# Delta rule in a two-layer network: the substitution of the diagonal blocks on GpSimd, fixed padded rows for the convolution, z's products tied to the inverse's last levels

## The chip, the cores and the metric

The kernel runs on one core of a Trainium2 chip. The metric is the time of the program on the device in microseconds (us). Three runs of the kernel before gave a median of 1310.2 us (1309.93 to 1312.19). Engines are called by their names in the profile: PE is TensorE's matmul side and PEld its weight loads, DVE is VectorE, ACT is ScalarE, POOL is GpSimd, SP is SyncE, which issues the loads of weights.

## The reference, cut to what matters

The whole program is a network with two mixers, several MLPs and a second block; the change lies in its first layer, a gated delta rule over 256 tokens, 8 heads of 128. There:

```python
proj = hn @ w_in                                   # q, k, v, z: 1024 columns each, and 16 gate columns
qkv = silu(causal_depthwise_conv(proj[..., :3 * DN_DIM], conv_w))
...
a_low = where(tri_strict, einsum('bhncd,bhnsd->bhncs', k_beta, k) * decay, 0.0)
a_mat = a_low + eye(c)
sol = triangular_solve(a_mat, rhs, lower=True, unit_diagonal=True)
...
o = rmsnorm(o, out_norm_g) * silu(z)
return o.reshape(b, t, DN_DIM) @ w_out
```

The triangular matrix needs k and the gates alone. The z columns are needed only where the output o is gated.

## The kernel before, in words

Everything of the delta rule is in `delta_net`. Its products with `w_in` run in three passes per weight tile (high and low halves of the fp32 operands), through `lin`, `group` and `mm3`. A group of 512 columns takes 96 products of 128x128x256, fed by four chunks of weights of 512 KB; each chunk costs an ACT copy (`wh`, L76) and a DVE subtraction (`wl`, L56) in `split`. Names in rows: `acc<-xh,wh` and its two companions are these products; `ps` is any other bank of PSUM.

The stages, in the order of the text:

1. `gates`, `decays`, then `project` of k (two groups), `unit_keys` and `gram`. `gram` leaves in A, for 4 heads times 2 chunks of 128 rows, the triangular matrices.
2. `inverses`: the inverse Z of A starts from its 32x32 blocks on the diagonal. Four DMAs (L573) of POOL's queue bring those out to HBM (`ga`), two more (L576) bring them back one block per partition (`at`). 31 steps of substitution follow, each of them a product into `tmp` and a subtraction from `zt`, 62 TENSOR_TENSOR of DVE in all, each of which needs the one ahead of it. Then `zt` goes out (`gz`, L594, two DMAs) and back into the diagonal of Z (L597, four DMAs).
3. Two levels, `level_64` and `level_128`, each for the four pairs of g and c, join the blocks: four transposes of Z on PE (`turned`, L603), an ACT copy into X, small products of Z with A, an ACT copy into Y, products of Y with X, an ACT copy back into Z.
4. `project` of q and v. Each pair of 128 columns goes through `conv_pair`: ACT copies it behind three zeros in a tile `pad` of the rotating pool (L507 is the POOL memset of those zeros, made anew for every pair), and six DVE operations (`cy`, L59) add up the taps.
5. `intra` (products of q with k), `tokens` (transposes of k and v), and the generator `outputs`, a chain of products, ACT copies and DVE operations per half g.
6. The two groups of z, `lin(W, KD, [(3072, 512)], rd, on_z)` and the one at 3584, with `on_z`: a DVE operation, three ACT operations and another DVE operation per pair of columns, which release the bank of PSUM. At the end `residual_lin` multiplies by `w_out` (192 products, `acc<-xoh` and `acc<-xh`), then the MLP starts.

The order on each engine isn't that of the text: a scheduler takes, engine by engine, what it holds to be ready, by priority (the order of the text, put back by `later(n)`), and `after(...)` puts an instruction behind a named one. Each engine then runs its list in order. With two banks, `acc`, for the products with weights, a group's first product waits until `on_z` or the convolution has read the bank.

Of the kernel before, what the change touches and what calls it, by code (L numbers as in the profile page):

```python
# [8 lines left out]
F32 = mybir.dt.float32  # L9
# [3 lines left out]
OP = mybir.AluOpType  # L13
# [3 lines left out]
P = 128  # L17
T = 256
# [6 lines left out]
class Net:  # L25
# [420 lines left out]
    def delta_net(self):  # L446
        nc, tc, a = self.nc, self.tc, self.a
# [4 lines left out]
        with ExitStack() as ctx:  # L452
            dp = ctx.enter_context(tc.tile_pool(name="dn", bufs=1, reuse_waits="tile"))
# [45 lines left out]
            A = core.tile([P, 16, P], F32, name="A")  # L499
            Z = core.tile([P, 16, P], F32, name="Z")  # L500
            nc.gpsimd.memset(Z, 0.0)
            four = lambda t, g, c: t[:, (g * 2 + c) * 4:(g * 2 + c) * 4 + 4, :]

            def conv_pair(col, o, dst, behind):
                t = col // P
                pad = dp.tile([P, 2, T + 3], F32, tag="pad", name="pad", bufs=2)
                nc.gpsimd.memset(pad[:, :, 0:3], 0.0)  # L507
                self.copy(pad[:, :, 3:], o)
                y = dp.tile([P, 2, T], F32, tag="cy", name="cy", bufs=2)
                w = lambda j, i: cw[:, j * 24 + t + i:j * 24 + t + i + 1]  # L510
                for i in range(2):
                    self.act(y[:, i, :], o[:, i, :], AF.Copy, scale=w(3, i))
                for j in range(3):
                    for i in range(2):
                        self.stt(y[:, i, :], pad[:, i, j:j + T], w(j, i), y[:, i, :], OP.mult, OP.add)
                with self.after(*behind):
                    self.last_silu = self.act(dst, y, AF.Silu)

            def project(dst, tag, base, g, behind):
                dst[g] = dp.tile([P, 4, T], F32, tag=tag, name=tag, bufs=2)  # L520
                base += g * 512
                self.lin(W, KD, [(base, 512)], rd, lambda col, o: conv_pair(
                    col, o, dst[g][:, (col - base) // P:(col - base) // P + 2, :], behind))

            def big(tag, bufs, pool=None):
                return (pool or core).tile([P, 4, P], F32, tag=tag, name=tag, bufs=bufs)
# [39 lines left out]
            def inverses(sv):  # L566


                ga = hbm.tile([4, 16, 32, 32], F32, name="ga")
                gz = hbm.tile([4, 16, 32, 32], F32, name="gz")  # L570
                for b in range(4):
                    r = slice(32 * b, 32 * b + 32)
                    nc.gpsimd.dma_start(ga[b].rearrange("m i j -> i m j"), A[r, :, r])  # L573
                at = sv.tile([P, 32, 32], F32, name="at")
                for s in range(2):
                    nc.gpsimd.dma_start(at[s * 64:s * 64 + 64], ga.rearrange("b m i j -> (b m) i j"))  # L576
                zt = sv.tile([P, 16, 32], F32, name="zt")
                zi = sv.tile([P, 16, 32], I32, name="zi")
                nc.gpsimd.iota(zi, pattern=[[-2, 16], [1, 32]], base=0, channel_multiplier=0)
                zf = sv.tile([P, 16, 32], F32, name="zf")  # L580
                nc.gpsimd.tensor_copy(zf, zi)
                for s in range(2):
                    r = slice(s * 64, s * 64 + 64)
                    self.ts(zt[r], zf[r], float(s), None, OP.is_equal, eng=nc.gpsimd)
                tmp = sv.tile([P, 160], F32, name="tmp")
                for j in range(31):
                    n, m = j // 2 + 1, 31 - j
                    u = tmp[:, 0:n * m].rearrange("p (c i) -> p c i", i=m)
                    self.tt(u, zt[:, 0:n, j:j + 1].to_broadcast([P, n, m]),
                            at[:, j + 1:32, j][:, None, :].to_broadcast([P, n, m]), OP.mult)  # L590
                    self.tt(zt[:, 0:n, j + 1:32], zt[:, 0:n, j + 1:32], u, OP.subtract)
                to = gz.rearrange("b m (c s) i -> s (b m) c i", s=2)
                for s in range(2):
                    nc.gpsimd.dma_start(to[s], zt[s * 64:s * 64 + 64])  # L594
                for b in range(4):
                    r = slice(32 * b, 32 * b + 32)
                    nc.gpsimd.dma_start(Z[r, :, r], gz[b].rearrange("m c i -> c m i"))  # L597

            def turned(zz):
                X = big("X", 2)  # L600
                p = self.ps()
                for i in range(4):
                    nc.tensor.transpose(p[:, i * P:(i + 1) * P], zz[:, i, :], self.ident)  # L603
                self.copy(X, v4(p))
                return X

            def level_64(A, zz):

                X = turned(zz)
                v = lambda p, r: p[r:r + 32, 0:128].rearrange("p (h e) -> p h e", e=32)  # L610
                Y = big("Y", 2)
                p = self.ps()
                for r in (0, 64):
                    for i in range(4):
                        self.mm(p[r:r + 32, i * 32:(i + 1) * 32], A[r + 32:r + 64, i, r:r + 32],
                                zz[r + 32:r + 64, i, r + 32:r + 64], True, True)
                    self.copy(Y[r:r + 32, :, 0:32], v(p, r))
                p = self.ps()
                for r in (0, 64):
                    for i in range(4):  # L620
                        self.mm(p[r:r + 32, i * 32:(i + 1) * 32], X[r:r + 32, i, r:r + 32], Y[r:r + 32, i, 0:32],
                                True, True)
                    self.act(zz[r:r + 32, :, r + 32:r + 64], v(p, r), AF.Copy, scale=-1.0)
# [15 lines left out]
            def intra(g, c):  # L639

                cs = slice(c * P, (c + 1) * P)
                m = M[g, c]
                self.tt(m, m, b4(self.tri[:, 0:P]), OP.mult)
                p = self.ps()
                mm4(p, lambda i: (k[g][:, i, cs], q[g][:, i, cs]))
                self.tt(m, v4(p), m, OP.mult)
                if c == 1:
                    self.tt(qd[g], q[g][:, :, cs], qd[g], OP.mult)

            def tokens(g):  # L650

                h4 = slice(g * 4, g * 4 + 4)
                for c in range(2):
                    cs = slice(c * P, (c + 1) * P)
                    p = self.ps()
                    for i in range(4):
                        nc.tensor.transpose(p[:, i * P:(i + 1) * P], k[g][:, i, cs], self.ident)
                    kx[c] = big(f"kx{c}", 1, late)
                    self.tt(kx[c], v4(p), tok((beg if c else kdec)[:, h4]), OP.mult)
                    p = self.ps()  # L660
                    for i in range(4):
                        nc.tensor.transpose(p[:, i * P:(i + 1) * P], vt[g][:, i, cs], self.ident)
                    bv[c] = big(f"bv{c}", 1, late)
                    self.tt(bv[c], v4(p), tok(beta[:, c, h4]), OP.mult)
# [63 lines left out]
            both = [(g, c) for g in range(2) for c in range(2)]  # L728
# [12 lines left out]
            with tc.tile_pool(name="inv", bufs=1, reuse_waits="tile") as sv:  # L741
                inverses(sv)
            late = ctx.enter_context(tc.tile_pool(name="late", bufs=1, reuse_waits="tile"))
            for level in (level_64, level_128):
                for g, c in both:
                    level(four(A, g, c), four(Z, g, c))
            project(q, "q", 0, 0, behind)
            project(q, "q", 0, 1, behind)
            project(vt, "vt", 2048, 0, behind)
# [1 line left out]
            pin = self.table(self.last_silu)  # L751
            for g, c in both:
                intra(g, c)
            tokens(0)
            step = lambda it: next(it, None)
            out = [outputs(g) for g in range(2)]
            step(out[0])
            with self.later(300):
                self.lin(W, KD, [(3072, 512)], rd, on_z)
            step(out[0])  # L760
            step(out[0])
            xo[0] = (late.tile([P, 4, T], F32R, name="xoh"), late.tile([P, 4, T], F32R, name="xol"))
            with self.later(600):
                self.lin(W, KD, [(3584, 512)], rd, on_z)
            xo[1] = self.new_xg(0)
            tokens(1)
# [779 lines left out]
```

## Time and profile before

| | |
|---|---|
| median of 3 runs | 1310.2 us |
| the profiled execution | 1310.08 us, of it 1308.3 us span |
| PE busy | 1261.0 us (96%) |
| DVE busy | 867.1 us (66%) |
| ACT busy | 737.8 us (56%) |
| POOL busy | 20.9 us (2%) |
| TensorE clock granted, mean | 0.977 of full speed |
| chain that ended last: PE, DVE, ACT | 86%, 6%, 3% |

The profile is of one execution. Busy times of PE are modelled and overlap, so a busy PE isn't a PE at its peak. A clock of 1.00 in a row is 2.4 GHz, 0.50 is 1.2 GHz. The change touches the time from 71 to 230 us of the span; the stage tables below cut it where the work of PE changes: the rest of k's, all of q's and v's products (71.6 to 102.5), the first of z's (102.5 to 109.9), a stretch with the rest of z's (109.9 to 144.8), the two levels of the inverse (144.8 to 173.2), q with k (173.2 to 178.3), tokens and outputs (178.3 to 210), the rest of the products with `w_out` (210 to 229.8).

### The profile page before, as it was taken

Reading aid. Unit: us, or ns where it says so; the run is one execution under the profiler, and the core shown is the slowest. Engines: PE = TensorE matmul, PEld = TensorE weight load, DVE = VectorE, ACT = ScalarE, POOL = GpSimd, SP = SyncE. Lnnn points to the kernel's source line nnn. Section 1 sums busy time; section 2 is a strip of 40 time slices with the busy share of each in tenths; the row PEclk is TensorE's granted clock in tenths of the full one; section 3 lists DMA queues with packets and bytes.
Section 4 is the critical chain, followed back from the end, with each engine's and each line's share of the span. In section 5 each row is a group of like instructions: output and inputs, shape, how many; then the busy total and the mean of one; then the engine's idle time right before and its main releaser. Section 6 shows DMA issues by size and latency. Waiting matters only on the chain.

```text
span 1308.3 us, 23770 instructions
## 1 busy us (share of the span) xinstructions
PE 1261.0 (96%) x9674; PEld 1199.7 (92%) x9674; DVE 867.1 (66%) x1385; ACT 737.8 (56%) x1124; POOL 20.9 (2%) x68
## 2 busy tenths in 40 slices
PE   7997789999999999999999999999999998999998
PEld 6997688999999999999999987899999997999997
DVE  5799236644547666744546997998556685877775
ACT  5874536645546445755545644675447565656554
POOL 2010100000000000000000000000000000000000
PEclk8998689999999999999999999999999999999999
DMA  6454303666664744656652653446664654465652
GB/s 199 143 171 145 81 1 129 219 196 187 183 182 141 216 153 143 210 166 181 188 166 64 194 162 87 139 131 192 183 188 148 208 161 129 132 205 170 184 177 84
DMA packets 99633, 207.32 MB, mean 158 GB/s; under 512 B 9694, under 2 KB 12292, under 8 KB 99524
## 3 DMA queue, kind: packets, MB, share of 16 engines
q1 hardware_dynamic: 98114, 202.85, 50.7%
q0 software_dynamic: 928, 2.88, 0.8%
q8 instruction: 76, 1.25, 0.4%
q14 instruction: 33, 0.27, 0.1%
q10 hardware_dynamic: 482, 0.08, 0.0%
HBM read 204.21 MB, written 1.57 MB: 157 GB/s over the span
## 4 chain that ended last, share of the span: by engine, by line
PE 86%; DVE 6%; ACT 3%; issue 2%; DMA 2%; POOL 0%; DVEq 0%; SPq 0%; ACTq 0%; POOLq 0%
PE acc L53 53%; PE ps L53 32%; DVE wl L56 1%; ACT wh L76 1%; PE ps L603 1%; DVE cy L59 1%; DVE tmp L56 1%; PE ps L893 0%; DVE zt L56 0%; DVE sq L56 0%; DMA wr<-in_w_xkv_dram 0%; DMA xt<-in_x_dram 0%; DMA Z<-gz 0%; DMA gz<-zt 0%; DVE mx L879 0%
## 5 line engine op out<-in xcount | busy, mean ns | idle before, releaser
L56 DVE TENSOR_TENSOR wl<-wr,wh 128x1024 fp32r<-128x1024 f32 (+1 forms) x384 | 465.6, 1217 | 308.2 <-ACT wh L76 307.3
L76 ACT ACTIVATE wh<-wr 128x1024 fp32r<-128x1024 f32 (+1 forms) x384 | 402.3, 1052 | 394.3 <-PE acc L53 246.9
L53 PE MATMUL acc<-xh,wh 128*128 128x256 f32 (+1 forms) x1064 | 305.9, 288 | 7.8 <-DVE z L59 5.1
L53 PE MATMUL acc<-xh,wl 128*128 128x256 f32 (+1 forms) x1064 | 303.8, 286 | 3.5 <-DVE wl L56 3.5
L53 PE MATMUL acc<-xl,wh 128*128 128x256 f32 (+1 forms) x1064 | 304.4, 286 | 0.8 <-DVE xl L56 0.8
L53 PE MATMUL ps<-xh,wh 128*128 128x256 f32 (+1 forms) x872 | 248.5, 285 | 6.7 <-ACT xh L69 3.5
L53 PE MATMUL ps<-xl,wh 128*128 128x256 f32 (+1 forms) x872 | 248.2, 285 | 0.5 <-DVE xl L56 0.3
L53 PE MATMUL ps<-xh,wl 128*128 128x256 f32 (+1 forms) x872 | 248.0, 284 | 0.0
L53 PEld LDWEIGHTS acc<-xh,wh 128*128 128x128 f32 (+1 forms) x1064 | 204.4, 192 | 11.4 <-issue 6.5
L53 PEld LDWEIGHTS acc<-xh,wl 128*128 128x128 f32 (+1 forms) x1064 | 204.1, 192 | 6.0 <-DVE wl L56 3.7
L53 PEld LDWEIGHTS acc<-xl,wh 128*128 128x128 f32 (+1 forms) x1064 | 204.6, 192 | 3.2 <-issue 1.5
L53 PEld LDWEIGHTS ps<-xh,wh 128*128 128x128 f32 (+1 forms) x872 | 166.8, 191 | 8.4 <-ACT xh L69 3.9
L53 PEld LDWEIGHTS ps<-xl,wh 128*128 128x128 f32 (+1 forms) x872 | 166.9, 191 | 1.6 <-DVE xl L56 1.1
L53 PEld LDWEIGHTS ps<-xh,wl 128*128 128x128 f32 (+1 forms) x872 | 167.0, 192 | 0.3
L53 PE MATMUL acc<-hh,wh 128*128 128x256 f32 x512 | 144.6, 282 | 0.0
L53 PE MATMUL acc<-hh,wl 128*128 128x256 f32 x512 | 144.3, 282 | 0.0
L53 PE MATMUL acc<-hl,wh 128*128 128x256 f32 x512 | 144.2, 282 | 0.0
L53 PEld LDWEIGHTS acc<-hh,wl 128*128 128x128 f32 x512 | 97.3, 190 | 0.0
L53 PEld LDWEIGHTS acc<-hh,wh 128*128 128x128 f32 x512 | 97.2, 190 | 0.0
L53 PEld LDWEIGHTS acc<-hl,wh 128*128 128x128 f32 x512 | 97.1, 190 | 0.0
L59 DVE SCALAR_TENSOR_TENSOR yc<-cpad,vec_b,yc 128x256 f32<-128x256 f32 x120 | 51.6, 475 | 0.1
L59 DVE SCALAR_TENSOR_TENSOR fy<-pad,vec_b,fy 128x256 f32<-128x256 f32 x88 | 36.9, 478 | 0.1
(418 smaller groups left out, 1759.6 us busy)
## 6 DMA issues: line engine op xcount, KB each, us to landing
wr<-in_mlp_w_up_dram SPq DMA_DIRECT2D x64, 512.0 KB
wr<-in_mlp_w_down_dram SPq DMA_DIRECT2D x64, 512.0 KB
wr<-in_w_in_dram SPq DMA_DIRECT2D x44, 512.0 KB
wr<-in_w_up_dram SPq DMA_DIRECT2D x44, 512.0 KB
wr<-in_dn_w_in_dram SPq DMA_DIRECT2D x32, 512.0 KB
wr<-in_w_gate_dram SPq DMA_DIRECT2D x32, 512.0 KB
wr<-in_mb_w_in_dram SPq DMA_DIRECT2D x24, 512.0 KB
wr<-in_w_down_dram SPq DMA_DIRECT2D x22, 512.0 KB
```

What stands on the lines that cost most here:

```text
L53: return self.nc.tensor.matmul(out, lhsT=lhsT, rhs=rhs, start=start, stop=stop, skip_group_check=True)
L56: return (eng or self.nc.vector).tensor_tensor(out=out, in0=a, in1=b, op=op)
L59: self.nc.vector.scalar_tensor_tensor(out, a, s, b, op0=op0, op1=op1, **kw)
L76: a = self.nc.scalar.activation(hi, src, AF.Copy)
L603: nc.tensor.transpose(p[:, i * P:(i + 1) * P], zz[:, i, :], self.ident)
```

## The change

Three parts. The 62 operations of the substitution go to GpSimd. The two tiles `pad` are made once, their zeros are set once, and they are used in turn. The two levels are written behind `intra`, and the products of z may be issued only behind given transposes of them: the first group behind those of the first `level_64`, the second behind those of the first `level_128`.

```diff
             nc.gpsimd.memset(Z, 0.0)
+            pads = [dp.tile([P, 2, T + 3], F32, name=f"pad{i}") for i in range(2)]
+            for pad in pads:
+                nc.gpsimd.memset(pad[:, :, 0:3], 0.0)
...
-                pad = dp.tile([P, 2, T + 3], F32, tag="pad", name="pad", bufs=2)
-                nc.gpsimd.memset(pad[:, :, 0:3], 0.0)
+                pad = pads[t // 2 % 2]
...
                     self.tt(u, zt[:, 0:n, j:j + 1].to_broadcast([P, n, m]),
-                            at[:, j + 1:32, j][:, None, :].to_broadcast([P, n, m]), OP.mult)
-                    self.tt(zt[:, 0:n, j + 1:32], zt[:, 0:n, j + 1:32], u, OP.subtract)
+                            at[:, j + 1:32, j][:, None, :].to_broadcast([P, n, m]), OP.mult, nc.gpsimd)
+                    self.tt(zt[:, 0:n, j + 1:32], zt[:, 0:n, j + 1:32], u, OP.subtract, nc.gpsimd)
...
-                    nc.tensor.transpose(p[:, i * P:(i + 1) * P], zz[:, i, :], self.ident)
+                    self.last_turn = nc.tensor.transpose(p[:, i * P:(i + 1) * P], zz[:, i, :], self.ident)
...
-            for level in (level_64, level_128):
-                for g, c in both:
-                    level(four(A, g, c), four(Z, g, c))
             project(q, "q", 0, 0, behind)
...
                 intra(g, c)
+            turns = []
+            for level in (level_64, level_128):
+                for g, c in both:
+                    level(four(A, g, c), four(Z, g, c))
+                    turns.append(self.last_turn)
             tokens(0)
...
-            with self.later(300):
+            with self.later(300), self.after(turns[0]):
                 self.lin(W, KD, [(3072, 512)], rd, on_z)
...
-            with self.later(600):
+            with self.later(600), self.after(turns[4]):
                 self.lin(W, KD, [(3584, 512)], rd, on_z)
```

On POOL, from A to the way back of Z, the list reads before

```order
L573 DMA ga<-A 32x16x32 x4
L507 MEMSET pad 128x2x3 x2
L576 DMA at<-ga 64x1024 x2
L507 MEMSET pad 128x2x3 x3
L594 DMA gz<-zt 1024x1x32 x2
L597 DMA Z<-gz 32x16x32 x4
```

and now

```order
L575 DMA ga<-A 32x16x32 x4
L578 DMA at<-ga 64x1024 x2
L56 TENSOR_TENSOR tmp<-zt,at 128x31
L56 TENSOR_TENSOR zt<-zt,tmp 128x31
L56 TENSOR_TENSOR tmp<-zt,at 128x30
L56 TENSOR_TENSOR zt<-zt,tmp 128x30
```

The memsets between `ga` and `at` are gone, and behind `at` the 62 operations follow, each of which waits for the one ahead of it, up to `gz` and Z; three memsets stood there before.

On PE, at the first `level_64` (`ident,Z` are its transposes), the list reads before

```order
L53 MATMUL acc<-xh,wl 128x256
L603 MATMUL ps<-ident,Z 128x128 x4
L53 MATMUL ps<-Z,A 32x32 x8
L53 MATMUL ps<-Y,X 32x32 x4
L603 MATMUL ps<-ident,Z 128x128 x2
```

where the `acc` row is the last of 192 products of z, all of them ahead of the levels, and now

```order
L53 MATMUL acc<-xh,wl 128x256
L53 MATMUL ps<-q,k 128x128 x16
L605 MATMUL ps<-ident,Z 128x128 x4
L53 MATMUL ps<-Z,A 32x32 x4
L53 MATMUL acc<-xh,wh 128x256
L53 MATMUL acc<-xl,wh 128x256
L53 MATMUL ps<-Z,A 32x32 x4
L53 MATMUL ps<-Y,X 32x32 x4
```

where the first `acc` row is the last product of v, and the two behind the transposes are the first of z. The products of q with k, which stood behind the levels, now stand ahead of them; of z's 192 products, 38 stand inside the eight levels, in lots of 2, 5, 6, 6, 5, 6, 4 and 4, and 154 behind them, among the outputs and ahead of the products with `w_out`.

## Rows read from the trace of the kernel before

**Rows 1.** Busy time by stage, all engines: start:end, length, PE, PEld, DVE, ACT, POOL, clock, DMA
```profile
71.60:102.50 30.90, 30.80 (x255) 30.39 (x254) 29.91 (x71) 20.02 (x29) 4.43 (x11) 1.00 0.56 173
102.50:109.90 7.40, 7.32 (x59) 6.91 (x58) 7.40 (x21) 4.50 (x9) 0.00 (x0) 1.00 0.49 144
109.90:144.80 34.90, 20.43 (x140) 19.90 (x141) 26.62 (x54) 16.79 (x23) 4.25 (x6) 0.86 0.63 181
144.80:173.20 28.40, 24.51 (x225) 19.41 (x225) 0.75 (x1) 12.10 (x32) 0.00 (x0) 0.50 0.01 2
173.20:178.30 5.10, 5.10 (x33) 5.10 (x33) 2.04 (x3) 0.38 (x1) 0.00 (x0) 0.69 0.00 0
178.30:210.00 31.70, 29.44 (x221) 25.85 (x221) 15.96 (x25) 15.75 (x26) 1.22 (x3) 1.00 0.06 18
210.00:229.80 19.80, 17.41 (x144) 17.00 (x143) 16.30 (x24) 12.73 (x19) 0.00 (x0) 1.00 0.61 203
```

**Rows 2.** The chain that ended last, from the substitution's end to the levels: start, us, what
```profile
131.73 0.79 POOL gz L594
...
139.54 5.14 DMA Z<-gz
144.82 1.10 PE ps L603 x4
```

**Rows 3.** Waits of PE between 100 and 150 us: total, times, longest
```profile
PE ps L603 <- DMA Z<-gz: 5.9, 1, 5.9
...
PE acc L53 <- DVE z L59: 5.1, 2, 4.9
```

**Rows 4.** The substitution's two tiles, all instructions: durations in ns, first and last start
```profile
L56 DVE TENSOR_TENSOR tmp<-zt,at x31: 185/347/406, 87.9 to 131.0; 128x126 f32<-128x126 f32 x3, 128x30 f32<-128x30 f32 x2, 128x56 f32<-128x56 f32 x2, 128x78 f32<-128x78 f32 x2
L56 DVE TENSOR_TENSOR zt<-zt,tmp x31: 180/256/293, 88.6 to 131.2; 128x126 f32<-128x126 f32 x3, 128x30 f32<-128x30 f32 x2, 128x56 f32<-128x56 f32 x2, 128x78 f32<-128x78 f32 x2
```

**Rows 5.** Timeline of POOL, instructions that the terms rest on: start, us, what, [idle before]
```profile
1.90 0.61 POOL L581 CAST zf<-zi 128x512 f32<-128x512 int32 x1
2.60 3.05 POOL L64 TENSOR_SCALAR zt<-zf 64x512 f32<-64x512 f32 x2
...
73.91 2.83 POOL L573 DMA_DIRECT2D ga<-A  x4 [5.40 <-DVE A L59]
...
82.00 0.10 POOL L507 MEMSET pad<- 128x6 f32 x1 [5.15 <-DVE cy L59]
82.63 1.07 POOL L576 DMA_DIRECT2D at<-ga  x2 [0.53 <-issue]
...
205.57 0.69 POOL L144 CAST df<-di 128x384 f32<-128x384 int32 x1
```

**Rows 6.** DMA issues: queue, count, KB each, us from issue to landing
```profile
at<-ga POOLq DMA_DIRECT2D x2, 256.0 KB, 3.4
...
ga<-A POOLq DMA_DIRECT2D x4, 64.0 KB, 2.5
```

**Rows 7.** DVE by form, 83.2 to 112 us: count, busy us, mean ns, idle before
```profile
L59 DVE SCALAR_TENSOR_TENSOR cy<-pad,vec_a,cy 128x256 f32<-128x256 f32 x27 | 12.8, 478 | 0.3 <-ACT cy L69 0.3
L56 DVE TENSOR_TENSOR wl<-wr,wh 128x1024 fp32r<-128x1024 f32 x6 | 7.2, 1217 | 0.3 <-ACT wh L76 0.2
L56 DVE TENSOR_TENSOR m<-m,tri 128x512 f32<-128x512 f32 x4 | 2.7, 678 | 0.0
L56 DVE TENSOR_TENSOR qd<-q,qd 128x512 f32<-128x512 f32 x2 | 1.4, 676 | 0.0
```

**Rows 8.** Timeline of DVE beside the second CAST of rows 5
```profile
204.68 1.22 DVE L56 TENSOR_TENSOR wl<-wr,wh 128x1024 fp32r<-128x1024 f32 x1
```

**Rows 9.** The chain that ended last, one group of the MLP's products
```profile
302.38 11.44 PE acc L53 x96
```

**Rows 10.** Busy time in single microseconds of q's products with k
```profile
175.00:176.00 1.00, 1.00 (x7) 1.00 (x6) 0.69 (x1) 0.00 (x0) 0.00 (x0) 0.50 0.00 0
...
177.00:178.00 1.00, 1.00 (x12) 1.00 (x10) 0.80 (x2) 0.00 (x0) 0.00 (x0) 1.00 0.00 0
```

## The prediction

> **What bounds the kernel now.** I read the busy time by stage first, then the chain that ended last, then the waits, and took durations from the timelines and groups.
>
> PE bounds the program: one group of the MLP's products, 96 of them, takes 11.44 us [rows 9], which is 0.119 us a product, back to back, and nearly all of the span looks like that. The changed part is where it doesn't. Until 109.9 us PE is full [rows 1]; the reader sees 30.80 of 30.90 us busy and then 7.32 of 7.40. From 109.9 to 144.8 it is busy for 20.43 of 34.90 us: z's products are held up by a full DVE, and at the end nothing is left but to wait for Z, 5.9 us by the waits [rows 3]. The two levels take 28.4 us at a clock of 0.50, and in the next 5.1 us the clock is 0.69 on average [rows 1]. From there to the last product with `w_out` at 229.8 us PE idles for 2.3 and 2.4 us [rows 1]. So four stretches lose time: 14.5 us idle before Z, the levels at half clock, part of q with k, and 4.7 us behind.
>
> What sets the start of the levels is Z. DVE does the last subtraction at 131.2 us [rows 4], POOL issues `gz` at 131.73, the way back lands behind 139.54 + 5.14, and PE starts at 144.82 [rows 2]: 13.4 us from the end of the substitution to the levels, all of it DMA and issue.
>
> **The change, part by part.**
>
> *The padded rows.* POOL's last `ga` goes out one issue of 0.7 us before 73.91 + 2.83 us, at 76.0, and lands 2.5 us later, at 78.5 [rows 5, 6]. Before, POOL's list has a memset of `pad` in between that waits 5.15 us for a convolution, until 82.00, so that `at` is issued at 82.63 [rows 5]. Now `at` follows at about 78.7; its second half goes out 0.5 us later and lands after 3.4 us [rows 6], at 82.6, and with the 0.5 us that stood ahead of `at` [rows 5] the substitution can start at 83.2 instead of 87.9 us [rows 4]. The other memsets moved to the program's start cost POOL two times 0.1 us [rows 5], which nobody waits for. ACT's writes into `pad` wait only for the convolution two pairs earlier, as before.
>
> *The substitution on POOL.* 62 operations, each behind the one ahead; the 31 widths add up to 2856 elements per partition, twice that is 5712. No row shows a two-input operation of POOL. Per operation I take 0.19 us: 0.10 for a memset of 6 elements and 0.09 between the CAST's end at 2.51 and the start of the operation that needs it at 2.60 [rows 5]. Per element the nearest rows give 1.2 ns (a CAST of 512, 0.61 us) and 3.0 ns (TENSOR_SCALAR of 512, 3.05 us for two) [rows 5]. I take their middle, 2.1, and a third more for the half of the operations that read `at` in steps of a row, as DVE's medians of 347 and 256 ns have it [rows 4]: 2.4 ns. Alone: 62 x 0.19 + 5712 x 2.4 ns = 25.5 us, ends 18.6 and 28.9. On GpSimd, the Trainium skill's "GPSIMD Engine Reference" (section 3.1) gives 4497 ns for a two-input add of 2048, an estimate of 2.2 ns per element, by which the sum would be 24.3 us.
>
> It isn't alone. From 83.2 us on, DVE has to do 27 `cy`, 6 `wl`, 4 `m` and 2 `qd` [rows 7], 39 operations and 24.1 us, all with both inputs in SBUF. The one operation of POOL in this trace that reads SBUF beside DVE is a CAST of 384: 0.69 us [rows 5], longer than the one of 512 beside an idle DVE. It starts at 205.57, and DVE's `wl` runs from 204.68 to 205.90 [rows 8]. At the other's rate it would have taken 0.46; the 0.23 more are most of what `wl` still had to run. So I take it that the two engines take turns: between two operations of DVE goes one of POOL. Then 39 of POOL's operations pass while DVE works: 24.1 us and their own 3830 elements x 2.4 ns = 9.2 us, until 116.5 us; the other 23 take 23 x 0.19 + 1882 x 2.4 ns = 8.9 us. The substitution ends at 125.4 (118.6 with 1.2 ns, 128.8 with 3.0), Z is there 13.4 us later, at 138.8 (132 to 142.2).
>
> The Trainium skill's "SBUF — State Buffer" (section "Who interferes with whom") states it as a lock: a DVE instruction with two SBUF inputs and a GpSimd instruction that reads SBUF exclude each other, and the second one to issue waits for the whole of the first. The CAST agrees with it; taken instead as a CAST that is slow by itself, it leaves the first rival below, 1298.2 us.
>
> *DVE's relief.* The 62 operations leave DVE (18.7 us by the medians [rows 4]). It pays in full only from 109.9 on, where DVE is the one that is late; but there PE now has nothing to do but wait for Z, so I count nothing.
>
> *q with k ahead of the levels.* It used to run from 173.2 to 178.3 us, half of it at half clock. Now it fills 2 us at full clock of the wait for Z: minus 5.1 us behind the levels.
>
> *z in and behind the levels.* 38 products stand inside. At half clock one takes 0.238 us, together 9.0 us, of which PE's idle time there, 28.4 - 24.5 = 3.9 us [rows 1], hides as much: the levels would take 33.5 us. If the clock rises, PE's work is 24.5 / 2 + 38 x 0.119 = 16.8 us; with the 3.9 us of waits on ACT, which don't shrink, and some 3 us at the start until it rises, 23.5 us. I take the second: with q and k the clock was 0.50 in the third microsecond of a full PE and 1.00 in the fifth [rows 10], while the levels before, at 86% busy, stayed at 0.50 [rows 1]; z's products close just these gaps. The first stays as a bound.
>
> Behind the levels: before, 229.8 - 178.3 = 51.5 us. Add 154 products x 0.119 = 18.3. Subtract half of the 4.7 us of idle time, 2.3 (ends: none, all). Add the hand-over of the two banks: a group's first product waits for `on_z`, 5.1 us in two waits before [rows 3], which lay in the stretch ahead of Z; now they lie behind it (ends: 0, 5.1; I take all, since the order puts the second group and then `w_out` right behind). The sum is 72.6 us (65 to 75).
>
> **The sum.** 138.8 + 23.5 + 72.6 = 234.9 us against 229.8: 5.1 us later. What follows is the same list. The profiled execution took 1310.08 us (1308.3 of span and 1.8 around it), 0.1 under the median: **1315.2 us**. In words: Z comes 6 us earlier and the levels get 5 us shorter, but 16 us of z's products that ran while PE had to wait anyway now run where it doesn't.
>
> **The rivals.**
>
> *No turns: POOL at its own pace, and faster.* Substitution over at 83.2 + 25.5 = 108.7, Z at 122.1, levels to 145.6, end at 218.2: 11.6 us earlier, **1298.5 us**. For it: DVE slows by nothing in rows 8, and one CAST is thin evidence, of another type than the 62. Against it: rows 7 leave POOL hardly a gap. It decides where the substitution ends before 120 us: then Z at 133.7 and 23.5 + 72.6 give the old 229.8.
>
> *Turns, and the clock stays at 0.50 in the levels.* 138.8 + 33.5 + 72.6 = 244.9: 15.1 us later, **1325.2 us**. For it: PE was 86% busy there without a rise [rows 1], and the first level holds only 2 of z's products. Against it: rows 10.
>
> *No turns and half clock.* 122.1 + 33.5 + 72.6 = 228.2: 1.6 us earlier, **1308.5 us**, which no measurement tells from no change.
>
> That the order does something other than the diff says is excluded by the lists shown.
>
> **How the numbers follow.** Chances: the forecast 0.42, the faster rival 0.28, turns with half clock 0.18, no turns with half clock 0.12. A measurement tells 0.2%, 2.6 us, from no change. Within the forecast the end moves from 118.6 to 128.8 us in the substitution alone, minus 1.7 to plus 8.5 us on the total, and the tail adds minus 8 to plus 2: of its 0.42, 0.05 is faster, 0.08 the same and 0.29 slower. The faster rival gives 0.26 faster, 0.01 same and 0.01 slower; half clock with turns 0.18 slower; half clock without 0.05, 0.04 and 0.03. Sums: faster 0.36, same 0.13, slower 0.51. The range for 8 in 10 leaves out the fast half of the first rival's spread below 1296 (its 18.6 us end is 7 us earlier) and the slow end of the second above 1327: **1296 to 1327 us**. Both signs hold much of the chance; the forecast's own range is 1306 to 1322 us.
>
> **What would show it.** In the profile after: POOL's first `tmp` near 83 us; 62 operations that take some 42 us with gaps as long as DVE's operations (turns) or some 26 us (none); PE idle from about 106 us to Z; the levels' first transposes at 139 or at 122; the granted clock in the levels, 1.00 after the second one or 0.50; two waits of PE's `acc` on z behind the levels. If POOL's operations start to start take 0.4 us beside a busy DVE, the forecast is wrong at the turns; if the tail behind the levels is below 65 us, at the hiding of z.

## The result, and the profile after

The change makes the kernel slower: 1326.45 us (median of 4 runs, 1326.02 to 1327.88) against 1310.78, a ratio of 1.0123 with an interval of 1.0108 to 1.0138. The profiled execution has a span of 1324.9 us (before 1308.3). Predicted were 1315.2 us, with a range of 1296 to 1327, and, as the rival "turns, and the clock stays at 0.50 in the levels", 1325.2. The stages of after, cut where PE's work changes (start:end, length, PE, PEld, DVE, ACT, POOL, clock, DMA share, GB/s):

```profile
102.50:106.20 3.70, 3.53 (x32) 3.33 (x30) 3.70 (x5) 1.41 (x2) 3.44 (x4) 1.00 0.97 299
106.20:134.00 27.80, 0.00 (x0) 0.02 (x1) 9.52 (x15) 3.92 (x7) 19.70 (x42) 0.58 0.24 72
134.00:169.30 35.30, 35.29 (x266) 28.94 (x267) 1.23 (x1) 13.06 (x33) 0.00 (x0) 0.50 0.05 16
169.30:173.00 3.70, 3.70 (x23) 3.70 (x22) 2.77 (x4) 0.00 (x0) 0.00 (x0) 0.61 0.00 0
173.00:200.00 27.00, 26.24 (x201) 23.44 (x200) 8.39 (x11) 13.16 (x21) 1.04 (x3) 1.00 0.12 39
200.00:248.00 48.00, 41.54 (x302) 40.14 (x302) 35.77 (x48) 30.12 (x43) 0.00 (x0) 0.89 0.46 158
```

Against [rows 1] the reader sees three things. PE does nothing at all for 27.8 us ahead of the levels, where before it was busy for 20.43 of 34.90 us. In the levels PE is full, 35.29 of 35.30 us, and the clock is 0.50 all the same. Behind them there are two stretches more in which PE idles and then comes back at half clock; the same view, cut there:

```profile
199.00:203.00 4.00, 0.91 (x8) 0.74 (x7) 2.85 (x4) 2.68 (x4) 0.00 (x0) 0.99 0.17 67
203.00:207.00 4.00, 4.00 (x18) 2.97 (x17) 2.11 (x4) 3.08 (x6) 0.00 (x0) 0.59 0.42 135
216.00:220.00 4.00, 0.84 (x8) 0.64 (x6) 2.81 (x4) 2.83 (x4) 0.00 (x0) 1.00 0.81 294
220.00:226.00 6.00, 5.41 (x25) 5.44 (x26) 3.77 (x6) 3.36 (x6) 0.00 (x0) 0.50 0.34 121
```

PE's waits from 95 to 250 us (total, times, longest), which answer to [rows 3]:

```profile
PE ps L605 <- DMA Z<-gz: 28.0, 1, 28.0
PE acc L53 <- DVE z L59: 6.8, 2, 3.8
```

The substitution on POOL, the two tiles of [rows 4] (ns min/median/max, first and last start):

```profile
L56 POOL TENSOR_TENSOR tmp<-zt,at x31: 218/480/1361, 86.4 to 123.8; 128x126 f32<-128x126 f32 x3, 128x30 f32<-128x30 f32 x2, 128x56 f32<-128x56 f32 x2, 128x78 f32<-128x78 f32 x2
L56 POOL TENSOR_TENSOR zt<-zt,tmp x31: 228/443/1297, 87.3 to 124.1; 128x126 f32<-128x126 f32 x3, 128x30 f32<-128x30 f32 x2, 128x56 f32<-128x56 f32 x2, 128x78 f32<-128x78 f32 x2
```

PE's timeline at the first transposes of Z, the first transposes of k behind the levels, and the first product of the MLP:

```profile
134.01 1.09 PE L605 MATMUL ps<-ident,Z 128*128 128x128 f32 x4 [27.98 <-DMA Z<-gz]
...
168.42 1.11 PE L659 MATMUL ps<-ident,k 128*128 128x128 f32 x4
...
246.58 0.28 PE L53 MATMUL ps<-xh,wh 128*128 128x256 f32 x1
```

The list of what answers to the prediction's sum: the levels start at 134.0 us (before 144.8, predicted 138.8), the first transposes of k behind them at 168.4, so they take 34.4 us (before 28.4, predicted 23.5), and the MLP begins 78.2 us later, at 246.6 (before 229.8, predicted 72.6 us behind the levels). 134.0 + 34.4 + 78.2 is 16.8 us more than before; the spans differ by 16.6.

### The profile page after: what moved, and what is told of

Its sections match the earlier page's. It is cut to its first block, busy times and chain, and to the rows that moved or that the text cites. A ratio compares the mean times of both kernels' runs of the same rounds, so it can differ in the third digit from the quotient of the medians.

```text
span 1324.9 us, 23729 instructions
## 1 busy us (share of the span) xinstructions
PE 1265.1 (95%) x9674; PEld 1203.4 (91%) x9674; DVE 859.4 (65%) x1323; ACT 737.6 (56%) x1124; POOL 53.0 (4%) x120
## 4 chain that ended last, share of the span: by engine, by line
PE 74%; DVE 3%; ACT 2%; issue 1%; DMA 0%; DVEq 0%; ACTq 0%; SPq 0%
PE acc L53 47%; PE ps L53 27%; ACT wh L76 1%; DVE wl L56 0%; DVE xl L59 0%; PE ps L897 0%; DMA wr<-in_w_xkv_dram 0%; DVE sq L56 0%; DVE mx L883 0%; ACT s L69 0%; ACT pT L72 0%; DVE x L56 0%; ACT L69 0%; DVE s L59 0%; DVE y L59 0%
```

## The experiments

Each median stands beside that of the kernel before, run on the same chip (1310.3 to 1311.3 us). "Levels" are counted from the first transposes of Z to the first transposes of k, or to the last product `ps<-Y,X` where other work comes between. A diff shows the lines that matter; `...` marks lines left out.

**1. Which part costs?** Four kernels, each of which undoes or takes one part.

`e3`: the fixed pads alone; `inverses` on DVE, levels and z as before.

```diff
...
-                pad = dp.tile([P, 2, T + 3], F32, tag="pad", name="pad", bufs=2)
-                nc.gpsimd.memset(pad[:, :, 0:3], 0.0)
+                pad = pads[t // 2 % 2]
```

> The kernel before with the fixed padded rows alone. Theory: the transfer that brings the blocks back is issued some 4 us earlier, beside the weight loads, and lands as much later as in the changed kernel (7.0 us instead of 3.4), so the substitution starts about 1 us earlier: 1309 to 1311 us, no change. Rival (the prediction's own step: a start 4.7 us earlier): about 1306 us.

Measured: 1310.4 us, ratio 1.000 (0.9985 to 1.0014). The pads are worth nothing. The view of the tile `at` says why: it is issued at 78.5 us instead of 82.63 [rows 5], and takes as much longer to land, 7.3 us instead of 3.4 [rows 6].

```profile
L578 POOL DMA_DIRECT2D at<-ga x2: 529/538/547, 78.5 to 79.0; - x2
...
DMA to landing us min/median/max: 7.1/7.3/7.4
```

`e2`: the change with only the substitution put back on DVE.

```diff
-                            at[:, j + 1:32, j][:, None, :].to_broadcast([P, n, m]), OP.mult, nc.gpsimd)
-                    self.tt(zt[:, 0:n, j + 1:32], zt[:, 0:n, j + 1:32], u, OP.subtract, nc.gpsimd)
+                            at[:, j + 1:32, j][:, None, :].to_broadcast([P, n, m]), OP.mult)
+                    self.tt(zt[:, 0:n, j + 1:32], zt[:, 0:n, j + 1:32], u, OP.subtract)
```

> The change with the substitution put back on DVE, z bound and pads fixed; the list of PE is that of the change. Theory: GpSimd as such earns, since from 86.4 us on DVE has 24 us of convolution and weight splits and 18.7 us of substitution in one list, 43 us in all, against 38 us on GpSimd beside it: Z some 5 us later than in the change, about 1331 us (1326 to 1334). Rival (the turns of the two engines are the loss): the substitution is over before 120 us and the time falls below 1322.

Measured: 1327.98 us, ratio 1.0135 (1.0113 to 1.0157), against 1.0123 for the change. Neither theory's size holds: the two intervals overlap, so GpSimd's 1.5 us here aren't told from nothing, where the theory gave 5, and the turns lose nothing against DVE. The last subtraction starts at 125.1 us on DVE (the tile `zt`, in a run of 1332.0 us) and 124.1 on POOL, 131.2 before [rows 4]:

```profile
L56 DVE TENSOR_TENSOR zt<-zt,tmp x31: 182/266/303, 88.3 to 125.1; 128x126 f32<-128x126 f32 x3, 128x30 f32<-128x30 f32 x2, 128x56 f32<-128x56 f32 x2, 128x78 f32<-128x78 f32 x2
```

With the pads alone (e3) it starts at 131.1. So it wasn't GpSimd that brought Z forward, but that z's operations had left DVE.

`e1`: the change without the two bindings of z.

```diff
-            with self.later(300), self.after(turns[0]):
+            with self.later(300):
...
-            with self.later(600), self.after(turns[4]):
+            with self.later(600):
```

> The change without the two bindings of z's products (the later(300) and later(600) kept): by the list of PE 52 of the 192 then stand ahead of the levels, 44 inside and 96 behind, where the change has 0, 38 and 154. Theory: the change loses because z's products left PE's wait for Z (27.8 us idle there) for places where they cost PE time. 52 of them go back into the wait: 58 fewer behind the levels at 0.119 us are minus 6.9, 6 more inside at half clock plus 1.4, and one hand-over of the banks fewer behind, some minus 3: about 1318 us against the changed kernel's 1326.4. Rival (GpSimd and DVE taking turns is the loss, the binding plays no part): 1326, or more, since z's DVE work then runs beside the substitution.

Measured: 1314.7 us, ratio 1.0034 (1.0021 to 1.0047). The two bindings cost 11.7 us, more than the 8 expected. The levels are no shorter (136.7 to 172.3 us, at 0.50), so the gain is what lies behind them: from there to the MLP it is 63.7 us instead of 78.2, of which the 58 products fewer are 6.9.

`e4`: the levels written where they stood, ahead of q and v, and z unbound.

```diff
+            for level in (level_64, level_128):
+                for g, c in both:
+                    level(four(A, g, c), four(Z, g, c))
             project(q, "q", 0, 0, behind)
```

> Fixed pads and the substitution on GpSimd, but the levels written ahead of q and v and z unbound, as before: 83 of z's products stand ahead of the levels, the rest inside and behind, q with k behind the levels. Theory (what counts is how many products lie in the wait for Z): 83 products hidden are minus 9.9 us against the change, q with k behind plus 2 to 5, one hand-over fewer minus 3: about 1317 us (1312 to 1321). Rival (turns are the loss): z's DVE work beside the substitution makes it longer, and the time stays at 1326 or above.

Measured: 1318.9 us, ratio 1.0060 (1.0043 to 1.0076). As the theory had it, in size too. It is slower than before all the same, though its Z is there at 137.1 us instead of 144.8: 83 products in the wait are fewer than 192. It is slower than e1 too, with 52 in the wait, where q with k stands ahead of the levels; so the count of products isn't all.

**2. All of z in the wait.** `e5`: q with k, then z's 192 products, then the levels, bound behind the last of them.

```diff
+            self.lin(W, KD, [(3072, 512)], rd, on_z)
+            self.lin(W, KD, [(3584, 512)], rd, on_z)
+            with self.after(self.last_mm):
+                for level in (level_64, level_128):
+                    for g, c in both:
+                        level(four(A, g, c), four(Z, g, c))
...
-            with self.later(300), self.after(turns[0]):
-                self.lin(W, KD, [(3072, 512)], rd, on_z)
...
-            with self.later(600), self.after(turns[4]):
-                self.lin(W, KD, [(3584, 512)], rd, on_z)
```

> Fixed pads, the substitution on GpSimd, q with k ahead of the levels as in the change, but all 192 products of z ahead of the levels' first transposes. Theory: 192 products are 23 us at full clock and fit into the 27.8 us that PE idles; z's 8 weight splits and its evictions run on DVE beside the substitution, which then ends up to 6 us later than 124.4; Z at 134 to 140 us, levels 28.4 us as before, then 51.5 us behind them: 214 to 220 against 229.8 before, so 1294 to 1301 us. If the levels, right behind a full PE, keep the full clock, up to 10 us less. Rival (turns are the loss): the substitution is drawn out beyond 136 us by z's work and the time is 1307 us or more.

Measured: 1302.1 us, ratio 0.9936 (0.9921 to 0.9951): faster than both kernels, and 1 us above the theory's 1294 to 1301. The wait for Z and the levels, by the view of the stages:

```profile
109.90:138.10 28.20, 22.15 (x166) 21.89 (x164) 19.13 (x22) 13.29 (x17) 20.71 (x37) 0.88 0.49 143
...
138.10:141.20 3.10, 0.19 (x2) 0.01 (x1) 1.37 (x2) 1.57 (x2) 0.00 (x0) 1.00 0.87 233
141.20:170.30 29.10, 23.17 (x224) 18.69 (x224) 2.19 (x3) 14.27 (x36) 0.00 (x0) 0.53 0.06 20
```

Z is at 141.2, 1 us later than the theory's latest: the substitution ends at 128.8, but the way back takes 12.4 us, where in the change it takes 9.6. The DMA issues (KB each, us to landing) show it: in the change, without weights on the way,

```profile
Z<-gz POOLq DMA_DIRECT2D x4, 64.0 KB, 2.4
```

and in e5, beside the loads of the weights `w_out`, which run there before and in e5 and not in the change (DMA share 0.87 from 136.0 to 141.2 us, against 0.23 from 129.5 to 134.0),

```profile
Z<-gz POOLq DMA_DIRECT2D x4, 64.0 KB, 4.7
```

`e8`: e5 with the substitution on DVE (the diff of e2).

> e5 (all of z ahead of the levels) with the substitution on DVE. Theory (GpSimd earns where z's work is on DVE too, and nothing where it isn't): the substitution ends 2 to 6 us later than e5's 128.8, the total is 1304 to 1308 us. Rival (GpSimd is worth nothing here either, as with z bound, where 1328.0 stands against 1326.4): 1302 us.

Measured: 1309.96 us, ratio 0.9993 (0.9981 to 1.0005). GpSimd is worth 7 to 8 us here: the last subtraction starts at 132.8 us on DVE and at 128.5 on POOL (the tile `zt`, e8 and then e5),

```profile
L56 DVE TENSOR_TENSOR zt<-zt,tmp x31: 181/254/282, 88.3 to 132.8; 128x126 f32<-128x126 f32 x3, 128x30 f32<-128x30 f32 x2, 128x56 f32<-128x56 f32 x2, 128x78 f32<-128x78 f32 x2
...
L56 POOL TENSOR_TENSOR zt<-zt,tmp x31: 228/460/1301, 88.0 to 128.5; 128x126 f32<-128x126 f32 x3, 128x30 f32<-128x30 f32 x2, 128x56 f32<-128x56 f32 x2, 128x78 f32<-128x78 f32 x2
```

and the levels at 145.7 instead of 141.2. It earns where DVE has z's work too, as the theory said, and a little more than it gave: 4.5 us are the start of the levels, 1.1 the levels, and 2.4 lie behind them, where e8's mean clock is 0.92 and e5's 0.97.

**3. The clock in the levels.** `e7`: the change with unused products between q with k and the levels.

```diff
+            for _ in range(5):
+                p = self.ps()
+                for _ in range(12):
+                    with self.after(fill):
+                        fill = self.mm(p[:, 0:T], self.ones, self.tri, True, True)
```

> The change with 60 products of a 128x128 with a 128x256 operand in fp32 (some 26 us of PE at full clock, of which nothing is used) between q with k and the levels, so that PE doesn't idle in the wait for Z. Theory 'cold start' (the levels ran at half clock because PE had idled 27.8 us ahead of them): the clock stays at 1.00 in the levels, which take 20 to 25 us instead of 35.3: about 1313 us. Rival 'content' (levels and z's 38 products together don't bring or hold the full clock, whatever ran ahead): the clock is at 0.50 a few us into the levels, which take 33 to 35 us: 1324 to 1327 us.

Measured: 1321.2 us, ratio 1.0084 (1.0069 to 1.0099). Taken alone it speaks for "content": PE comes in at full clock, and it falls. But the filling ended 2.4 us too early:

```profile
106.40:132.40 26.00, 26.00 (x122) 22.59 (x120) 9.85 (x16) 4.08 (x7) 19.51 (x42) 1.00 0.24 73
132.40:134.80 2.40, 0.04 (x1) 0.01 (x1) 0.00 (x0) 0.00 (x0) 0.54 (x1) 1.00 0.32 80
134.80:168.60 33.80, 33.77 (x269) 27.92 (x269) 1.23 (x1) 12.63 (x32) 0.00 (x0) 0.54 0.05 17
...
136.00:138.00 2.00, 2.00 (x27) 1.50 (x27) 0.00 (x0) 0.78 (x5) 0.00 (x0) 0.83 0.00 0
138.00:140.00 2.00, 2.00 (x22) 1.94 (x22) 0.00 (x0) 1.13 (x3) 0.00 (x0) 0.50 0.00 0
```

`e13`: 66 of them instead of 60 (`range(6)` and `range(11)`), nothing else.

> As the filled wait of e7, with 66 unused products instead of 60, so that they end at 135.0 us, when Z is there (134.8), and PE doesn't idle the last 2.4 us; the levels then hold 44 of z's products. Theory (what lets the clock fall is an idle stretch at the levels' start; a PE that comes into them without one, with z's products in the gaps, keeps 1.00, as in e10): the levels take 21 to 23 us instead of 35 and the total is e7's 1321.2 less 12 to 13, about 1308 us. Rival (e10 kept its clock for another reason, its two groups of z ahead): the clock is at 0.50 from the third microsecond of the levels, 1320 to 1322 us.

Measured: 1307.9 us, ratio 0.9976 (0.9964 to 0.9987).

```profile
106.40:135.00 28.60, 28.60 (x136) 25.14 (x135) 9.99 (x16) 4.13 (x7) 20.13 (x43) 1.00 0.25 78
135.00:155.80 20.80, 20.80 (x270) 17.34 (x268) 1.23 (x1) 12.51 (x32) 0.00 (x0) 1.00 0.08 27
```

This settles it. The same 268 products in the same order take 33.8 us at a clock that falls, and 20.8 at one that stays; the two kernels differ by the 2.4 us in which PE idled ahead of them. 13.0 us of levels are the 13.3 us between the medians, and the runs don't overlap: the four of e7 took 1319.9 to 1322.0 us at mean clocks of 0.978 to 0.980, the seven of e13 1305.7 to 1308.4 at 0.990 to 0.996. What the change lost in the levels is thus the cold start behind 27.8 us without work.

`e9`: e5 with the levels bound behind z's 144th product and the second group of z put back by `later(300)`. The trace has the other 48 products ahead of the levels' last `ps<-Y,X`, so 48 stand inside, not 44.

```diff
-            with self.after(self.last_mm):
+            with self.after(self.mms[47]):
```

> e5 with the levels tied behind z's 144th product instead of the last: by the list of PE 144 products ahead of the levels, 44 inside, 4 behind. Theory 'cold start': PE comes hot into the levels and z's products close the gaps, so the clock stays at 1.00, the levels take some 20 us instead of 29.2: about 1293 us. Rival 'content': 0.50 in the levels, which take 35 us; Z lands up to 3 us earlier with fewer weight loads beside it: 1304 to 1308 us, slower than e5.

Measured: 1308.0 us, ratio 0.9966 (0.9936 to 0.9997), in two lots: eight runs from 1306.7 to 1311.1 at a mean clock of 0.972 to 0.978, two at 1294.1 and 1294.5 at 0.988 and 0.987. The profile is of the first lot:

```profile
132.50:140.60 8.10, 0.04 (x1) 0.00 (x0) 1.23 (x1) 1.02 (x1) 2.59 (x4) 0.71 0.59 165
140.60:176.70 36.10, 36.05 (x273) 30.12 (x273) 3.44 (x5) 15.45 (x36) 0.00 (x0) 0.50 0.05 16
```

PE idles 8.1 us, the clock falls in it, and full levels don't bring it back: 0.50 all through. `e10` closes that wait:

```diff
+            fill = self.mms[47]
+            p = self.ps()
+            for _ in range(20):
+                with self.after(fill):
+                    fill = self.mm(p[:, 0:T], self.ones, self.tri, True, True)
+            with self.after(fill):
-            with self.after(self.mms[47]):
```

> e9 with 20 unused fp32 products (some 8 us) between z's 144th product and the levels, which fill PE's 8.1 us of waiting for Z. Of e9's ten runs two took 1294.3 us, at a mean clock of 0.987 instead of 0.975. Theory (the clock at the entrance into the levels splits e9's runs): the clock stays at 1.00 in the levels and all runs are near 1294 us. Rival (as in e7, the clock falls a few us into the levels though PE comes hot): 1305 to 1308 us.

Measured: 1293.97 us (1293.21 to 1295.48), ratio 0.9869 (0.9855 to 0.9884), the fastest of all, and as the theory had it:

```profile
131.60:140.10 8.50, 8.50 (x41) 7.43 (x40) 1.23 (x1) 1.02 (x1) 2.59 (x4) 1.00 0.62 162
140.10:161.40 21.30, 21.30 (x274) 17.82 (x272) 3.19 (x4) 14.59 (x36) 0.00 (x0) 1.00 0.07 27
```

`e11`: e5 with 8 unused products in the last wait and 10 in each level.

```diff
...
+                        p = self.ps()
+                        for _ in range(10):
+                            with self.after(self.last_turn):
+                                self.mm(p[:, 0:T], rd(0)[0][:, 0:P], rd(1)[0], True, True)
```

> e5 with 8 unused fp32 products (3.3 us) in the last wait for Z and 10 unused products of 128x128x256 in f32r in each of the eight levels, bound behind its transposes. Theory 'density' (the levels fall to half clock because most of their products are small; enough full-size products between them hold the clock): the clock stays at 1.00, the levels take 18 to 21 us instead of 29.2: 1292 to 1295 us. Rival (it falls all the same): the 80 products at half clock are 19 us less the 5 us of gaps: 1313 to 1317 us.

Measured: 1307.4 us (1302.3 to 1313.1 in six runs), ratio 0.9978 (0.9949 to 1.0007); it isn't told from before. Neither theory holds whole: in the profiled execution (1302.28 us) the clock is held, and yet the levels, from 141.5 to 170.6 us, take no less than e5's 29.1 us at half clock:

```profile
142.50:172.00 29.50, 24.94 (x294) 21.74 (x295) 0.75 (x1) 12.93 (x35) 0.00 (x0) 1.00 0.04 12
```

The mean clock is 0.989 to 0.992 in the three shorter runs and 0.981 to 0.986 in the three longer ones, so it wasn't held in all. Why a full clock gains nothing here can be read from PE's waits in the levels:

```profile
PE ps L53 <- ACT Y L72: 4.6, 8, 1.0
```

In e10 z's products stand where PE would wait for ACT's copy Y, and it waits nowhere; here the unused ones stand behind that wait, which stays. 21.3 us of e10 less 48 x 0.119 for z's products, plus 80 x 0.119 for the unused ones, plus 4.6 are 29.7.

**4. The tail.** `e12`: the change with four banks for the products with weights.

```diff
-        banks.enter_context(self.banks(2))
+        banks.enter_context(self.banks(4))
```

> The change with four banks of PSUM for the products with weights instead of two (and four for the rest instead of six). Theory (the two waits of 3.8 and 3.0 us behind the levels, and the fall of the clock behind each of them, are the hand-over of two banks): PE doesn't idle at 199.5 and 216.8 us, the clock stays at 1.00 there, and the total is 10 to 12 us less than 1326.4: 1314 to 1317 us. Rival (DVE's list is late, whatever the banks): 1325 to 1328 us; the levels may lose a few us to having four banks.

Measured: 1320.5 us, ratio 1.0071 (1.0054 to 1.0088), half of what the theory gave. One of the two waits is gone, the other is not, and the clock falls behind it as before (PE's waits, then the stages):

```profile
PE acc L53 <- DVE z L59: 3.8, 1, 3.8
```

```profile
220.00:224.00 4.00, 1.53 (x11) 1.36 (x11) 2.82 (x5) 1.76 (x4) 0.00 (x0) 0.89 0.53 164
224.00:228.00 4.00, 3.75 (x17) 3.75 (x18) 2.27 (x4) 2.33 (x5) 0.00 (x0) 0.50 0.00 2
```

So the banks are the cause of the first wait; the second, between z's last product and the next of `w_out`, is another thing, and stays open.

## Why the prediction was right, and where its sizes were off

The direction and its reason held: z's products went from a wait to places where PE pays for them. e1 and e5 show it: with 0, 52 and 192 products in the wait (and the levels behind q with k) the total is 1326.4, 1314.7 and 1302.1 us. The number is right by its range alone, and by little: 1326.45 us lies 0.5 us inside the end of 1327, which was set by a rival with a chance of 0.18, and outside the forecast's own 1306 to 1322. That this rival's 1325.2 us came so near is luck in part: its levels of 33.5 us were right, but it has Z 4.8 us too late and 5.6 us too little behind the levels, and the two cancel. The sum of 5.1 us, measured 16.8, was made of one step that failed, the clock in the levels, and of sizes that missed, some of them against each other.

- *The start of the substitution*, put at 83.2 us, was 86.4. The step took the 3.4 us to landing [rows 6] along with an issue that it moved 4.3 us forward, into denser weight loads (DMA share 0.85 from 78.3 to 86.4 us, where before 82.6 to 87.9 had 0.63); there it was 7.0. e3 confirms it: no gain. The prediction costed the issue as if the duration belonged to the transfer.
- *The turns of the two engines* were right in their order and too dear in their price. By the timelines, DVE does 36 operations with both inputs in SBUF from 86.4 to 112.1 us, and POOL 37 of its own, one for one. The Trainium skill's "SBUF — State Buffer" (section "Who interferes with whom") has each side blocked for the whole of the other's instruction; the trace agrees on POOL's side, beside a long operation of DVE. Beside DVE's `wl` an operation of POOL takes 1.3 us, beside an idle DVE 0.4 (timeline of POOL):

```profile
101.11 1.34 POOL L56 TENSOR_TENSOR tmp<-zt,at 128x120 f32<-128x120 f32 x1
102.52 1.30 POOL L56 TENSOR_TENSOR zt<-zt,tmp 128x120 f32<-128x120 f32 x1
...
117.07 0.43 POOL L56 TENSOR_TENSOR tmp<-zt,at 128x108 f32<-128x108 f32 x1
117.58 0.40 POOL L56 TENSOR_TENSOR zt<-zt,tmp 128x108 f32<-128x108 f32 x1
```

  On DVE's side it doesn't (timeline of DVE, then its groups from 98 to 113 us):

```profile
90.66 6.17 DVE L59 SCALAR_TENSOR_TENSOR cy<-pad,vec_a,cy 128x256 f32<-128x256 f32 x12
104.83 7.33 DVE L59 SCALAR_TENSOR_TENSOR cy<-pad,vec_a,cy 128x256 f32<-128x256 f32 x12
...
L59 DVE SCALAR_TENSOR_TENSOR cy<-pad,vec_a,cy 128x256 f32<-128x256 f32 x12 | 7.3, 681 | 0.0
L56 DVE TENSOR_TENSOR wl<-wr,wh 128x1024 fp32r<-128x1024 f32 x4 | 5.7, 1471 | 0.0
```

  Twelve turns of a `cy` and an operation of POOL take 6.2 and 7.3 us, 0.51 and 0.61 each, where `cy` without POOL takes 0.47 [rows 7] and POOL's operations there last 0.4 to 0.6. The means of 681 and 1471 ns, against 478 and 1217 [rows 7], make it look dearer than it is: the operations overlap, and twelve of 681 ns fit into 7.3 us. The prediction added both engines' times, 33.3 us for 39 turns; 36 took 25.7. The other 23 operations it had at 8.9 us; the last 25 took 12.3. (The first 39 operations have 3950 elements, not 3830, and the rest 1762, which leaves its sum as it is.)

- *GpSimd's own pace* was near: 0.51 us from start to start at 108 elements, where 0.19 + 108 x 2.4 ns makes 0.45. The substitution took 38.0 us instead of 42.2 and ended at 124.4 instead of 125.4: an end so near is luck, since turns that were cheaper made up for a start 3.2 us late and a slower rest. The credit was misplaced, though: on DVE it would have ended 1 us later (e2).
- *The way back of Z*, 13.4 us from [rows 2], was 9.6. Those rows were taken beside the loads of `w_out`, which the same change moves away from there, behind z's products; e5, which has them there again, gives 12.4. With the substitution's end this makes the levels begin 4.8 us before the forecast.
- *The levels* are the step that failed: "I take the second", the clock rises, 23.5 us. They took 34.4, at 0.50. The evidence, q with k [rows 10], was the wrong neighbour: there the clock rises, but in the levels, with PE full, it didn't rise in 34 us. The bound of 33.5 us, kept for the rival, was the right one. The prediction's reason was that z's products close the gaps of a PE that is 86% busy [rows 1]; they closed them, 35.29 of 35.30 us, and the clock stayed at 0.50. The other value exists too: 20.8 us in e13, where PE comes in without a gap; the prediction never asked what 27.8 us of idle time ahead of the levels do to the clock in them. (Its terms, 16.8, 3.9 and 3 us, add up to 23.7.)
- *The tail* was 78.2 us instead of 72.6. The two waits cost 6.8 us instead of 5.1; only the first of them is the hand-over of banks (e12). The rest is the clock, which no step had: 4.00 us of PE's work at 0.59 and 5.41 at 0.50 behind the two waits would have been 4.3 us shorter at 1.00.

134.0 + 34.4 + 78.2 against 138.8 + 23.5 + 72.6: minus 4.8, plus 10.9, plus 5.6, together the 11.7 us by which the forecast's execution missed.

## What to carry to other kernels

Work that is pulled out of a wait has to be priced where it lands, and the wait that it leaves behind has a price too: PE goes cold in it (0.58 on average in the change's 27.8 us), and what came next here, the levels, ran at half clock for all of their 34.4 us although they filled PE. Bringing the awaited result forward and keeping the filling in the wait are two changes; here the one alone lost, both together won (e5), and with the last idle stretch closed by products of no use the same levels fell from 29.1 us to 21.3 with 48 of z's products in them (e10). A landing time or a duration read from a trace belongs to the traffic beside it; ask whether the change moves that traffic as well.

## What the runs showed of the hardware that I had not expected

- A PE without a gap stayed at 0.50 for 34.4 us in the levels (products of 32x32, 64x64 and 128x128 mixed with z's), while the same mix with six more of z's, entered at full clock without a gap, stayed at 1.00 for 20.8 us. The list of e13 with 2.4 us of idle time ahead of the levels (e7) came in at 1.00 and was at 0.50 from 138 us on; in e5, too, 2.9 us of idle time came ahead of the fall.
- DMA landings moved with the weight loads by a factor of two in this kernel: `at` 3.4 or 7.0 us (DMA share 0.63 or 0.85), Z 2.4 or 4.7 (0.23 or 0.87).
- The substitution on POOL isn't free for DVE: beside it a `cy` comes every 0.51 to 0.61 us instead of 0.47, a `wl` every 1.41 instead of 1.20. It is far from the sum of both engines' times.
- One program can have two times: e9's runs fall into 1294 and 1308 us, with mean clocks of 0.987 and 0.975. With the wait filled, in e10, all four came out at 1294; that e9's two short runs kept their clock through the levels as e10 does is argued from that, since no profile is of them. If they did, on the same list, an idle stretch doesn't bring the clock down each time.
